# Moving two splits of returned head outputs into the last query projection, and head 0's fetches to GpSimd's queue

## The chip, the cores and the metric

The kernel runs on one core of a Trainium2 chip. The core has five engines with a queue of instructions each, which they work through in order: TensorE (PE, matrix products), VectorE (DVE), ScalarE (ACT), GpSimd (POOL) and SyncE (SP, which here only issues transfers). Transfers between HBM and the on-chip memory are issued from the queues of SP, ACT and POOL. The metric is the time of one execution on the device in microseconds, the median of several runs.

## The reference

One layer of a decoder trunk on 512 tokens of width 2048, in float32: a sparse-attention mixer with 16 heads of 128 in 4 groups, a gated feed-forward of width 5632, and three norms.

```python
def nsa_mixer(h, rel_bias, w_in, w_out, ...):
    proj = h @ w_in
    q, kc, vc, ks, vs, kw, vw, gl = jnp.split(proj, bounds, axis=-1)
    ...
    o = (gates[:, :, 0, :, :, None] * o_c + gates[:, :, 1, :, :, None] * o_s
         + gates[:, :, 2, :, :, None] * o_w)
    return o.reshape(Bsz, S, N_HEADS * DH) @ w_out

def swiglu(h, w_in, w_out):
    z = h @ w_in
    a, b = z[..., :D_FF], z[..., D_FF:]
    return (jax.nn.silu(a) * b) @ w_out

    h = x
    h = h + nsa_mixer(rmsnorm(h, mix_norm_g[0]), ...)
    h = h + swiglu(rmsnorm(h, ffn_norm_g[0]), ffn_w_in[0], ffn_w_out[0])
    return rmsnorm(h, final_norm_g)
```

The three branches of the attention (compressed, selected, window) each have a softmax per head and are summed with gates. With 8 blocks of 64 tokens and 16 to select, the selected branch takes all blocks.

## The kernel before

**Precision.** Every float32 operand of a large product is kept as two float32r parts, high and low. A *split* makes them: ScalarE copies the value into the high part, VectorE subtracts that from the value to get the low part. A product is then three matmuls (`three`, lines 266 to 269): high times high (L267), L268 and L269. At L268 one low part enters, at L269 the other. Weights are split by `Weights.split` (ScalarE L97, VectorE L98) a few tiles ahead of their use. Three raw weight tiles exist; a tile's next load is issued when its split has read it (L81).

**Stages.** First the projections of keys and values of group 0 and of the first two heads' queries. Then the attention stage (about 200 to 700 us of the span), whose outer loop runs over the 16 heads `h` with 12 steps `i` each (line 881). Then the rest of the output projection, the second norm and the feed-forward.

**The attention stage** interleaves two streams in program order, and the engines' in-order queues follow that order:

- *The head stream* (vector work mostly). For head `h + 1`, `scores` (line 781) makes the scores of one tile of 128 queries on TensorE, VectorE adds the bias and finds the maximum (L803), ScalarE takes the exponential (L805). `finish` (line 808) scales the weights by gate and sum (L810 to L817), transposes them in blocks on VectorE (L818), and stores them to HBM in four transfers (L820). `fetch(t)` (line 822) brings the tile `t` back as `PT` with the key index on the partitions (L824). For head `h`, `turn` (line 831) splits a piece of `PT` (ScalarE L841, VectorE L845 or L843), and `values` (line 848) multiplies it with the values of the head's group into `o`. `head_out` (line 861) parks the outputs of heads 0 to 11 in HBM (`d_o`, L866); from head 12 on they are split straight into the slots of `hn_h` and `hn_l` (L292, L293).
- *The dense stream* (`dense`, line 734; TensorE mostly): query, key and value projections of the coming heads and groups, and at its end four `partial` products (line 706), each of which multiplies the outputs of heads 0 to 11 with 256 columns of the output weights. `pump` (line 748) takes pieces of this stream after each step of the head stream, until a goal in TensorE time is reached; `drain_to` takes what a head needs.

Nothing else orders the work: no scheduler moves instructions. In this stage weights are loaded from GpSimd's queue (`W.queue = pool`, line 871), bias tables, stores and fetches go through SP's.

**The outputs coming back.** The normed input lies in `hn_h` and `hn_l`, 16 slots of 128 channels each. The last query projection, `qpair(14)` (line 653), runs over four chunks `i` of four slots; each chunk has two halves of four pieces, and after each piece the generator yields (`n` counts 0 to 7). When a chunk is done with, its slots are free, and `reload_o` (line 697) brings one parked output into a slot of `hn_l` from GpSimd's queue: outputs 0 to 2 in chunk 1, 3 to 5 in chunk 2, 6 to 8 in chunk 3, and 9 to 11 in the first `partial`. `split_o(k)` (line 701) splits the slots 2k and 2k + 1 in place: a copy on ScalarE (L703, 128 x 1024), then a subtraction on VectorE (L704). The `partial` products read slots 0 to 3 with their first weight tile (`i` = 0), 4 to 7 with the second and 8 to 11 with the third, each for the four token tiles `t` in turn, slot by slot.

Splits 0 and 1 stand behind the whole chunk 3 of `qpair(14)`, 2 and 3 in the first weight tile of the first `partial` ahead of its token tiles 1 and 3, and 4 and 5 in the second likewise. In program order of the time before, the copies of splits 0, 1 and 2 follow each other directly on ScalarE, behind the copy of the last query half (L292).

**The queues around head 0.** Before the loop over heads, lines 874 to 880 make the scores of head 0, tile 3 first, with `fetch(3)` and `fetch(2)` between the `finish` of the tiles; `fetch(1)` and `fetch(0)` follow in steps 0 and 2 of head 0. For later heads the fetches stand in steps 8, 11 and 2.

Of the kernel before, what the change touches and what calls it, by code (L numbers as in the profile page):

```python
# [19 lines left out]
S, D, H, DH, G, HPG = 512, 2048, 16, 128, 4, 4  # L20
# [20 lines left out]
PT_STEP = 224  # L41
# [132 lines left out]
def nsa_block(ctx: ExitStack, tc: tile.TileContext, x, rel_bias, mix_g, ffn_g, fin_g, w_in, w_out,  # L174
              pos_k, w1k, w2k, pos_v, w1v, w2v, f_in, f_out, onehot, out):
    nc = tc.nc
    mm, act, dve, pool = nc.tensor.matmul, nc.scalar.activation, nc.vector, nc.gpsimd
# [27 lines left out]
    def tok(t):  # L205
        return slice(128 * t, 128 * (t + 1))
# [59 lines left out]
    def three(o, ah, al, bh, bl, start, stop):  # L266
        mm(o, ah, bh, start=start, stop=False, skip_group_check=True)  # L267
        mm(o, ah, bl, start=False, stop=False, skip_group_check=True)  # L268
        mm(o, al, bh, start=False, stop=stop, skip_group_check=True)  # L269

    def ws(ps, gi, g, c0=0, c1=S, start=None, end=None, of=None):

        for u in range(2):
            cs = slice(128 * u, 128 * (u + 1))
            if end and gi == 3 and u:
                W.ahead(3)
            for k in range(4):
                kk = 4 * gi + k
                st = (kk == 0) if start is None else (start and kk == 0)
                three(ps[u][:, c0:c1], g[0][:, k, cs], g[1][:, k, cs],  # L280
                      *(x[:, kk, c0:c1] for x in of or (hn_h, hn_l)), st, kk == KC - 1)
                if end and gi == 3 and k == 3:
                    end(u)
                yield 650
# [57 lines left out]
    def q_out(ps, h0):  # L342
        def end(u):
            Q[h0 + u] = tuple(qp.tile([128, S], F32R, name=f"q{n}") for n in "hl")
            split_from(normed(ps[u], SCALE), Q[h0 + u][0], Q[h0 + u][1])

        return end
# [282 lines left out]
    with ExitStack() as st2:  # L630
# [3 lines left out]
        runs = [32 * (2 * t + 3) for t in range(NT)]  # L634
        P = [ap_.tile([128, 4, runs[t]], F32, name=f"p{t}", bufs=1) for t in range(NT)]
        CX = [ap_.tile([128, 32], F32, name=f"cx{t}", bufs=1) for t in range(NT)]
        PT = ap_.tile([128, 4, PT_STEP * 3 + runs[3]], F32, name="ptr", bufs=1)
        d_p = [dram.tile([4, 32, 4, runs[t]], F32, name=f"d_p{t}") for t in range(NT)]
# [5 lines left out]
        def stage_tile():  # L644
            return ap_.tile([128, 1024], F32, name="stage", bufs=1)
# [3 lines left out]
        def proj2():  # L649
            pool_ = (psx, ps2)[next(units) % 2]  # L650
            return [pool_.tile([128, 512], F32, name="proj") for _ in range(2)]

        def qpair(h0):
            ps = proj2()
            end = q_out(ps, h0)
            for i in range(4):
                last = ws(ps, i, W.take(), end=end)
                for n, c in enumerate(last):
                    yield c
                    if h0 == H - 2 and i and n in (2, 4, 6):  # L660
                        reload_o(3 * i + n // 2 - 4)
                if h0 == H - 2 and i == 3:
                    split_o(0)
                    split_o(1)
            done["n"] += 1
            yield None

# [29 lines left out]
        def reload_o(i):  # L697

            pool.dma_start(hn_l[:, i].bitcast(F32), d_o[i // 4][i % 4])

        def split_o(k):
            h, l = (x[:, 2 * k:2 * k + 2] for x in (hn_h, hn_l))
            act(h, l.bitcast(F32), AF.Copy)  # L703
            dve.tensor_tensor(l, l.bitcast(F32), h.bitcast(F32), op=OP.subtract)  # L704

        def partial(cb):
            st = stage_tile().rearrange("p (t c) -> p t c", t=NT)
            c = slice(256 * cb, 256 * (cb + 1))
            ps = [p.rearrange("p (t c) -> p t c", t=2) for p in proj2()]
            for i in range(3):  # L710
                w = W.take()
                if i == 1:
                    pool.dma_start(st, x[:, c].rearrange("(t p) c -> p t c", p=128))
                for t in range(NT):
                    if not cb and i == 0 and t < 3:
                        reload_o(9 + t)
                    if not cb and i < 2 and t % 2:
                        split_o(2 + 2 * i + t // 2)
                    if i == 2 and t == 2:
                        W.ahead(3)  # L720
                    for k in range(4):
                        h = 4 * i + k
                        three(ps[t // 2][:, t % 2], hn_h[:, h, tok(t)], hn_l[:, h, tok(t)], w[0][:, k], w[1][:, k],
                              h == 0 and t % 2 == 0, h == 11)
                        if k % 2:
                            yield 650
                    if i == 2 and t % 2:
                        b = t // 2
                        dve.tensor_tensor(st[:, 2 * b:2 * b + 2], st[:, 2 * b:2 * b + 2], ps[b], op=OP.add)
            pool.dma_start(d_h[:, c].rearrange("(t p) c -> p t c", p=128), st)  # L730
            done["n"] += 1
            yield None
# [15 lines left out]
        def pump(h, step):  # L748
            at = h + (step + 4) / STEPS
            goal = 20800 * min(at, 13) + 22500 * max(at - 13, 0)  # L750
            while done["ns"] < goal:
                c = next(stream, "end")
                if c == "end":
                    return
                done["ns"] += c or 0

        def drain_to(n):
            while done["n"] < n:
                c = next(stream, "end")
                if c == "end":  # L760
                    return
                done["ns"] += c or 0

        def needed(h):

            return 4 * ((h - 2) // 4) + (1 if h % 4 > 1 else 3) if h > 1 else 0
# [4 lines left out]
        def load_bias(h):  # L771
            if h < H:
                TB[h] = ap_.tile([128, S], F32, name="tb")
                (nc.sync if h else pool).dma_start(TB[h], bass.AP(tensor=d_u.tensor, offset=d_u.offset + h * UL + 127,
                                                 ap=[[H * UL - 1, 128], [1, S]]))
# [32 lines left out]
        def finish(h, t):  # L808
            r = HS[h]["sm"][:, t]
            dve.reciprocal(r, r)  # L810
            dve.tensor_mul(r, r, gates[:, t, h])
            for i, p in enumerate(HS[h].pop(t)):
                o = p
                if not i:
                    o = P[t][:, :3, runs[t] - 32:]
                    p = CX[t].unsqueeze(1).to_broadcast([128, 3, 32])
                dve.tensor_scalar(o, p, r[:, i:i + 1], None, op0=OP.mult)  # L817
            dve.transpose(P[t], P[t])  # L818
            for i in range(4):
                nc.sync.dma_start(d_p[t][:, :, i].rearrange("j a r -> a j r"), P[t][32 * i:32 * (i + 1)])  # L820

        def fetch(t):

            nc.sync.dma_start(PT[:, :, PT_STEP * t:PT_STEP * t + runs[t]], d_p[t].rearrange("j a i r -> (j a) i r"))  # L824

        def arrived(rows, c0, t0, step):
            v = PT[:rows, :, c0:c0 + 32]
# [46 lines left out]
        for i in range(4):  # L874
            scores(0, 3 - i)
            if i > 1:
                fetch(5 - i)
            if i:
                finish(0, 4 - i)
            pump(-1, min(9 + i, 11.7))  # L880
        for h in range(H):
            seq = [(b, kt) for kt in (3, 2, 1, 0) for b in (0, 1)] + [(-1, 0)]
            for i in range(STEPS):
                if i == 4:
                    load_bias(h + 2)
                if i == 2:
                    fetch(0)
                if i < 9:
                    turn(h, *seq[i])
                if i == 8 and h + 1 < H:  # L890
                    fetch(3)
                    fetch(2)
                if i == 11 and h + 1 < H:
                    fetch(1)
                if i == 0:
                    if not h:
                        fetch(1)
                    finish(h, 0)
                if h + 1 < H:
                    if i == 2:  # L900
                        drain_to(needed(h + 1))
                    if i % 3 == 2:
                        scores(h + 1, 3 - i // 3)
                    elif i % 3 == 0 and i:
                        finish(h + 1, 4 - i // 3)
                if 2 <= i < 10 or i == 11:
                    if i == 2 and h % HPG == 0:
                        drain_to(h)
                    values(h, *seq[min(i - 2, 8)])
                    if i == 11:  # L910
                        head_out(h)
                pump(h, i)
# [503 lines left out]
    n, na, pending = 0, 1, None  # L1416
# [88 lines left out]
```

## Time and profile before

| | us |
|---|---|
| median of 3 runs | 2143.42 (2141.70 to 2144.41) |
| profiled execution | 2139.23 |
| its span, from the first to the last instruction | 2137.5 |
| busy in it: TensorE, VectorE, ScalarE, GpSimd | 2104.2, 1634.8, 929.3, 132.5 |
| mean granted clock of TensorE | 0.994 of full speed |

A row of the profile's timeline has the start in us, the duration in us, the engine, the line of the kernel, the operation, what it writes and reads with shapes, how many like instructions are merged in the row, and in brackets the idle time of the engine before it with what ended it. "issue" there means that the profile shows no releaser. Rows of waits read: who waited for whom, us in total, how often, the longest. Rows of windows give the busy time of PE, weight loads, DVE, ACT and POOL, the granted clock, the share of the transfer engines in use and GB/s. Rows of transfers give the destination and source, the queue, the size and the median time from issue to landing. A transfer that SP issues shows as SPq.

### The profile page before, as it was taken

The page shows a single profiled execution, that of the slowest core. Times are in us where ns is not written, and L with a number is a line of the kernel's source. Part 1 is how long each engine was busy: PE and PEld are TensorE (multiplying, and loading weights), DVE is VectorE, ACT ScalarE, POOL GpSimd, SP SyncE. Part 2 cuts the span into 40 slices and gives each one's busy share as a digit, 9 for nine tenths or more (in the row PEclk, how much of TensorE's full clock was granted, in tenths as well). Part 3 has the DMA queues.
Part 4 walks back from the last instruction along what each step waited for, and adds up shares of the span by engine and source line. Part 5 has one row for each costly group of instructions (what it writes and reads, how often), then busy time and mean ns, then how long its engine had stood idle before and what let it go on. Part 6 is the DMA issues. An engine that isn't in the chain of part 4 may idle for free.

```text
span 2137.5 us, 37178 instructions
## 1 busy us (share of the span) xinstructions
PE 2104.2 (98%) x14697; PEld 1950.6 (91%) x14697; DVE 1634.8 (76%) x2674; ACT 929.3 (43%) x1439; POOL 132.5 (6%) x218
## 2 busy tenths in 40 slices
PE   9999999999989999999999999999999999999998
PEld 7898788898979889899999999999999888999896
DVE  5565777777777357898888888888888787877785
ACT  5344455555544234444444343443434444544344
POOL 1000011111121000000000000000000000001000
PEclk9999999999999999999999999999999999999999
DMA  6555667666667633344433334333343776878894
GB/s 218 177 160 152 178 191 200 193 195 192 194 214 226 229 134 113 117 131 128 129 126 122 122 125 129 129 119 127 121 129 129 258 276 219 297 268 312 300 330 153
DMA packets 272012, 388.08 MB, mean 182 GB/s; under 512 B 34668, under 2 KB 204700, under 8 KB 271197
## 3 DMA queue, kind: packets, MB, share of 16 engines
q1 hardware_dynamic: 245932, 275.52, 40.8%
q0 software_dynamic: 24000, 105.98, 14.3%
q10 hardware_dynamic: 1904, 4.20, 0.5%
q8 instruction: 115, 1.88, 0.4%
q14 instruction: 61, 0.49, 0.1%
HBM read 320.52 MB, written 70.36 MB: 183 GB/s over the span
## 4 chain that ended last, share of the span: by engine, by line
PE 65%; DMA 2%; DVE 2%; ACT 1%; issue 1%; SPq 0%; POOL 0%; ACTq 0%; DVEq 0%; POOLq 0%
PE f L268 18%; PE f L269 18%; PE f L267 18%; PE proj L269 1%; PE proj L268 1%; PE proj L267 1%; PE pp L269 1%; PE pp L268 1%; PE pp L267 1%; PE po L269 1%; PE po L267 1%; PE po L268 1%; DMA al<-d_s 1%; DMA d_p<-p 1%; DMA tt<-d_a 0%
## 5 line engine op out<-in xcount | busy, mean ns | idle before, releaser
L98 DVE TENSOR_TENSOR wlo<-raw,whi 128x1024 fp32r<-128x1024 f32 (+1 forms) x226 | 270.7, 1200 | 115.2 <-ACT whi L97 115.0
L97 ACT ACTIVATE whi<-raw 128x1024 fp32r<-128x1024 f32 (+1 forms) x226 | 234.5, 1040 | 223.6 <-DVE raw L1004 122.8
L1004 DVE TENSOR_TENSOR tlo<-tt,thi 128x1536 fp32r<-128x1536 f32 (+2 forms) x135 | 197.1, 1460 | 110.2 <-ACT thi L1106 89.0
L267 PE MATMUL f<-hn_h,whi 128*128 128x256 f32 x984 | 271.7, 276 | 0.8 <-ACT E L1064 0.8
L269 PE MATMUL f<-hn_h,wlo 128*128 128x256 f32 x984 | 271.6, 276 | 0.0
L268 PE MATMUL f<-hn_l,whi 128*128 128x256 f32 x984 | 271.6, 276 | 0.0
L1101 ACT ACTIVATE whi<-raw 128x1024 fp32r<-128x1024 f32 x123 | 126.0, 1057 | 292.2 <-DVE raw L1004 282.0
L267 PE MATMUL proj<-hn_h,whi 128*128 128x512 f32 x512 | 205.3, 401 | 0.4 <-ACT hn_h L402 0.4
L268 PE MATMUL proj<-hn_l,whi 128*128 128x512 f32 x512 | 201.5, 394 | 0.3 <-DVE hn_l L403 0.3
L269 PE MATMUL proj<-hn_h,wlo 128*128 128x512 f32 x512 | 201.5, 394 | 0.0
L267 PEld LDWEIGHTS f<-hn_h,whi 128*128 128x128 f32 x984 | 184.7, 188 | 1.2 <-ACT E L1064 1.2
L269 PEld LDWEIGHTS f<-hn_h,wlo 128*128 128x128 f32 x984 | 184.7, 188 | 0.0
L268 PEld LDWEIGHTS f<-hn_l,whi 128*128 128x128 f32 x984 | 184.7, 188 | 0.0
L1106 ACT ACTIVATE thi<-tt 128x1536 fp32r<-128x1536 f32 x82 | 121.9, 1487 | 84.2 <-PE f L268 84.2
L267 PE MATMUL proj<-whi,hn_h 128*128 128x256 f32 (+2 forms) x496 | 147.1, 297 | 6.8 <-ACT hn_h L703 6.8
L269 PE MATMUL proj<-whi,hn_l 128*128 128x256 f32 (+2 forms) x496 | 146.4, 295 | 2.9 <-DVE hn_l L704 2.9
L1004 DVE TENSOR_TENSOR wlo<-raw,whi 128x1024 fp32r<-128x1024 f32 x123 | 147.0, 1223 | 0.0
L268 PE MATMUL proj<-wlo,hn_h 128*128 128x256 f32 (+2 forms) x496 | 145.9, 294 | 0.0
L269 PE MATMUL f<-whi,tlo 128*128 128x512 f32 x320 | 124.9, 390 | 0.6 <-DVE tlo L1004 0.6
L268 PE MATMUL f<-wlo,thi 128*128 128x512 f32 x320 | 125.0, 391 | 0.0
L267 PE MATMUL f<-whi,thi 128*128 128x512 f32 x320 | 124.7, 390 | 0.0
L269 PEld LDWEIGHTS proj<-hn_h,wlo 128*128 128x128 f32 x512 | 97.0, 189 | 21.9 <-DVE wlo L98 0.2
(327 smaller groups left out, 6107.2 us busy)
## 6 DMA issues: line engine op xcount, KB each, us to landing
raw<-in_ffn_w_in SPq DMA_DIRECT2D x135, 512.0 KB, 3.6
raw<-in_ffn_w_out SPq DMA_DIRECT2D x88, 512.0 KB, 5.8
rawx<-in_ffn_w_in SPq DMA_DIRECT2D x41, 512.0 KB, 4.8
rawx<-d_a SPq DMA_DIRECT2D x31, 512.0 KB, 5.0
ah<-d_s POOLq DMA_DIRECT2D x16, 896.0 KB, 6.9
al<-d_s POOLq DMA_DIRECT2D x16, 896.0 KB, 9.5
raw<-in_nsa_w_in SPq DMA_DIRECT2D x24, 512.0 KB, 4.6
raw<-in_nsa_w_in POOLq DMA_DIRECT2D x24, 512.0 KB, 4.9
```

The costliest lines, as they stand in the source:

```text
L97: self.nc.scalar.activation(hi[:, :n], src, AF.Copy)
L98: self.nc.vector.tensor_tensor(lo[:, :n], src, hi[:, :n].bitcast(F32), op=OP.subtract)
L267: mm(o, ah, bh, start=start, stop=False, skip_group_check=True)
L268: mm(o, ah, bl, start=False, stop=False, skip_group_check=True)
L269: mm(o, al, bh, start=False, stop=stop, skip_group_check=True)
L1004: dve.tensor_tensor(o, a, b, op=OP.subtract)
L1101: act(h, r, AF.Copy)
L1106: act(h, ttf, AF.Copy)
```

## The change

```diff
@@ qpair
                     if h0 == H - 2 and i and n in (2, 4, 6):
                         reload_o(3 * i + n // 2 - 4)
-                if h0 == H - 2 and i == 3:
-                    split_o(0)
-                    split_o(1)
+                    if h0 == H - 2 and i == 3 and n in (0, 3):
+                        split_o(n // 3)
@@ partial
-                    if not cb and i < 2 and t % 2:
+                    if not cb and i < 2 and t % 2 == 0:
                         split_o(2 + 2 * i + t // 2)
@@ fetch
-        def fetch(t):
-
-            nc.sync.dma_start(PT[:, :, PT_STEP * t:PT_STEP * t + runs[t]], d_p[t].rearrange("j a i r -> (j a) i r"))
+        def fetch(t, queue=nc.sync):
+
+            queue.dma_start(PT[:, :, PT_STEP * t:PT_STEP * t + runs[t]], d_p[t].rearrange("j a i r -> (j a) i r"))
@@ the scores of head 0, and the loop over heads
             if i > 1:
-                fetch(5 - i)
+                fetch(5 - i, pool)
...
                 if i == 2:
-                    fetch(0)
+                    fetch(0, nc.sync if h else pool)
...
                     if not h:
-                        fetch(1)
+                        fetch(1, pool)
```

Splits 0 and 1 are issued inside chunk 3 of the last query projection, after its pieces 0 and 3. Splits 2 to 5 are issued one token tile earlier in the first `partial`, at its token tiles 0 and 2. The four fetches of head 0 are issued from GpSimd's queue, in the same places of the program; there they stand among the weight loads of line 81, which are issued in the same stage. All other fetches stay on SP's queue. No work is added or removed, and TensorE's instructions keep their order.

## The prediction

> **What bounds the kernel now.** I read the busy times first, then TensorE's waits by name, then the stretch that holds the longest of them, engine by engine in order of time.
>
> ```profile
> span 2137.5 us, 37178 instructions
> PE 2104.2 (98%) x14697; PEld 1950.6 (91%) x14697; DVE 1634.8 (76%) x2674; ACT 929.3 (43%) x1439; POOL 132.5 (6%) x218
> ...
> PE proj L267 <- ACT hn_h L703: 6.8, 2, 6.2
> PE proj L269 <- DVE hn_l L704: 2.9, 2, 2.1
> ```
>
> TensorE is busy 98% of the span, so a change can gain only its idle 2137.5 - 2104.2 = 33.3 us, plus time in which it runs slowly. The largest named waits are the two that the change aims at: 6.8 + 2.9 = 9.7 us for the splits of lines 703 and 704. Two more waits, 2.58 and 0.84 us (rows below), belong to head 0, whose fetches move.
>
> The stretch with the splits on TensorE, then its clock there (columns: PE, PEld, DVE, ACT, POOL busy, granted clock, DMA share, GB/s):
>
> ```profile
> 611.66 0.58 PE L267 MATMUL proj<-whi,hn_h 128*128 128x256 f32 x1 [6.22 <-ACT hn_h L703]
> 614.55 0.58 PE L269 MATMUL proj<-whi,hn_l 128*128 128x256 f32 x1 [2.09 <-DVE hn_l L704]
> 619.40 0.28 PE L267 MATMUL proj<-whi,hn_h 128*128 128x256 f32 x1
> 625.52 0.39 PE L269 MATMUL proj<-whi,hn_l 128*128 128x256 f32 x1 [0.76 <-DVE hn_l L704]
> 632.93 0.28 PE L269 MATMUL proj<-whi,hn_l 128*128 128x256 f32 x1
> 641.65 0.44 PE L268 MATMUL o<-ptl,v1h 128*128 128x384 f32 x1 [0.21 <-DVE ptl L845]
> ...
> 606.00:612.00 6.00, 0.34 (x1) 0.34 (x2) 4.88 (x15) 4.28 (x11) 3.41 (x6) 0.76 0.77 270
> 612.00:618.00 6.00, 3.91 (x18) 3.62 (x18) 4.73 (x6) 1.50 (x2) 0.00 (x0) 0.50 1.03 368
> ```
>
> TensorE is through with the last query projection at 611.66 - 6.22 = 605.4, stands still to 611.7 for split 0, again to 614.6 for its low part, and then runs at half clock (0.50) until 619.4. While it stands still, VectorE is busy 4.88 of 6 us: that queue is what the splits must pass.
>
> **The change part by part.** Edit 1 adds and removes no work: the same six copies and six subtractions come earlier in the in-order queues of ScalarE and VectorE. TensorE's own order stays as it is. What each displaces must be followed there:
>
> ```profile
> 604.89 0.63 ACT L292 ACTIVATE qh<-yt 128x512 fp32r<-128x512 f32 x1 [4.00 <-DVE yt L319]
> 605.43 1.04 ACT L97 ACTIVATE whi<-raw 128x1024 fp32r<-128x1024 f32 x1
> ...
> 603.58 0.68 DVE L845 TENSOR_TENSOR ptl<-ptr,pth 128x512 fp32r<-128x512 f32 x1
> 604.17 0.68 DVE L319 SCALAR_TENSOR_TENSOR yt<-proj,ybc 128x512 f32<-128x512 f32 x1
> 606.50 1.23 DVE L98 TENSOR_TENSOR wlo<-raw,whi 128x1024 fp32r<-128x1024 f32 x1 [0.25 <-ACT whi L97]
> 613.31 3.45 DVE L704 TENSOR_TENSOR hn_l<-hn_l,hn_h 128x1024 fp32r<-128x1024 f32 x3
> 621.36 0.19 DVE L803 CUSTOM_DVE_ANT_0 cx<-s,biasc 128x31 f32<-128x31 f32 x1 [4.60 <-PE s L269]
> 629.74 1.22 DVE L704 TENSOR_TENSOR hn_l<-hn_l,hn_h 128x1024 fp32r<-128x1024 f32 x1
> 631.38 0.43 DVE L845 TENSOR_TENSOR ptl<-ptr,pth 128x256 fp32r<-128x256 f32 x1 [0.42 <-issue]
> ```
>
> *Split 0* now stands before the L845 of 603.58. Its subtraction costs 3.45 / 3 = 1.15 there, so L845 starts at 604.73 and TensorE's matmul on it waits about 0.6 us; L319 starts at 605.32. TensorE enters the partial product at 605.9 without waiting for split 0.
>
> *Split 1* follows the L292 that L319 releases. L292 started 0.72 after L319 (604.89 - 604.17) and released ScalarE 0.54 later (605.43 - 604.89): 605.32 + 0.72 + 0.54 = 606.58, the copy (1.04, as the one of equal size at 605.43) ends at 607.62, the subtraction starts at 607.65. TensorE got going 1.24 after such a start (614.55 - 613.31), so here at 608.89.
>
> *What is pushed back.* Behind split 1, L98 starts at 607.65 + 1.15 = 608.80 instead of 606.50: 2.30 later, and so do the end of the last query projection and the finishing of head 13's second tile, which lie on VectorE up to 613.31. Split 2's subtraction therefore starts at 613.31 + 2.30 = 615.61, and TensorE, which would be there at about 614.4 (45 matmuls after 608.89 at 0.12, the mean of the 60 or so between 625.52 and 632.93), waits to 616.85. Also behind that L98 stands GpSimd's queue:
>
> ```profile
> 597.09 1.60 POOL L699 DMA_DIRECT2D hn_l<-d_o  x3
> 608.02 0.76 POOL L81 DMA_DIRECT2D raw<-in_nsa_w_out  x1 [2.55 <-DVE wlo L98]
> 608.77 2.66 POOL L699 DMA_DIRECT2D hn_l<-d_o  x5
> ...
> hn_l<-d_o POOLq DMA_DIRECT2D x1, 256.0 KB, 5.3
> ...
> L699 POOL DMA_DIRECT2D hn_l<-d_o x12: 537/539/552, 589.7 to 610.9; - x12
> ...
> DMA to landing us min/median/max: 4.5/5.9/7.1
> ```
>
> Outputs 2 and 3, which split 1 reads, are issued by 598.7 at the latest and landed 7.1 later at most, 605.8: no wait. The weight load of 608.02 waits for L98, and the last five reloads queue behind it. Output 7 goes out at 608.77 + 2.30 = 611.07 and lands 5.3 later, at 616.37 (4.5 to 7.1: 615.6 to 618.2). *Split 3* needs it: its copy ends at 617.45, its subtraction starts at 617.50, TensorE passes at 618.74. The copy now waits on ScalarE ahead of the exponentials of head 13's last tile and of head 12's output, and VectorE ahead of their first step (L803): a late output 7 holds them all, one for one. Before, this matmul ran at 625.52: 6.8 us gained, for the moment.
>
> *Splits 4 and 5.* VectorE's L803 follows split 3 at 617.50 + 1.15 = 618.65. From L803 to the L845 of 631.38 it took 10.02; without the idle 0.42 there and without split 3's subtraction inside (1.15) it takes 8.45. So L845 starts at 627.10 and split 5's subtraction 1.22 earlier, 625.88; TensorE has its result 1.24 later, at 627.12, where it would have been at 618.74 + (632.93 - 625.52) = 626.15: a wait of 1.0, and a lead of 632.93 - 627.12 = 5.8. VectorE itself leads by 631.38 - 627.10 = 4.3 only. At 641.65 TensorE already waited 0.21 for VectorE, so there its lead falls to VectorE's. Edit 1: **-4.3 us**. Where the stall goes: out of TensorE's 605 to 619, partly into new waits at splits 1, 2, 3 and 5 and at that L845.
>
> Its bounds: output 7 one way or the other gives -4.3 - 0.7 (split 3 right behind split 2, at 616.76) to -4.3 + 1.8. A clock that drops again after 618.74 is a rival below.
>
> *Edit 2*, head 0's fetches. Columns of the engine rows as above; SPq is the sync queue's issue:
>
> ```profile
> 216.46 1.11 DVE L818 STREAM_TRANSPOSE p<-p 128x896 f32<-128x896 f32 x1
> 218.50 0.61 SPq L824 DMA_DIRECT2D ptr<-d_p  x1
> 219.21 2.00 SPq L820 DMA_DIRECT2D d_p<-p  x4
> 223.99 0.44 PE L267 MATMUL o<-pth,v0h 128*128 128x128 f32 x1 [2.58 <-issue]
> 229.18 0.42 ACT L841 ACTIVATE pth<-ptr 128x256 fp32r<-128x256 f32 x1 [5.09 <-DMA ptr<-d_p]
> 237.57 0.44 PE L268 MATMUL o<-ptl,v0h 128*128 128x384 f32 x1 [0.84 <-DVE ptl L845]
> 246.45 1.04 ACT L97 ACTIVATE whi<-raw 128x1024 fp32r<-128x1024 f32 x1
> 224.00:227.00 3.00, 3.00 (x9) 2.50 (x10) 1.88 (x8) 0.09 (x1) 0.00 (x0) 0.50 0.64 206
> ```
>
> The first fetch waits on the sync queue for its stores, and the next tile's four stores, ready at 217.57, go out only at 219.21. With the fetch on GpSimd's queue they go out 1.6 us earlier, and the second fetch, which waits for them, as well; what waited for it at 229.18 moves up by 1.6 too, which covers the 0.84 us that TensorE waits at 237.57. The first fetch gains nothing: its own stores set its start. It costs what a GpSimd issue costs over a sync issue:
>
> ```profile
> tb<-d_u POOLq DMA_DIRECT2D x1, 256.0 KB, 3.4
> ...
> tb<-d_u SPq DMA_DIRECT2D x1, 256.0 KB, 3.9
> ...
> raw<-in_nsa_w_in SPq DMA_DIRECT2D x1, 256.0 KB, 2.9
> ...
> raw<-in_nsa_w_in POOLq DMA_DIRECT2D x1, 256.0 KB, 4.4
> ...
> L81 POOL DMA_DIRECT2D raw<-in_nsa_w_in x68: 747/749/764, 221.5 to 566.6; - x68
> ```
>
> The same table row took 0.5 less from GpSimd, a weight load 1.5 more; the tiles fetched here are nearer to the first pair in shape, the load around them nearer to the second: I take 0, bounds -0.5 to +1.5. The weight loads queued behind the second fetch on GpSimd go out some 2 us later (about 223.6), land within 4.4, and are first read by the third copy from there, at 246.45: free, with 18 us of cover; without it they would cost their delay one for one. Edit 2: **-0.8 us**, from -1.3 to +0.7.
>
> [...]
>
> Sum: -4.3 - 0.8 = -5.1 us. The profiled execution took 2139.23 us (span and 1.7 around it), 4.2 below the median of 2143.42; the terms are differences inside it, so they go onto the median: **2138.3 us**.
>
> **The rivals.** *B, half the gain is given back* (0.21). The pauses before 616.85 and 618.74 add up to about 3.7 us within 4.4; one pause of 2.58 before 223.99 was enough for a clock of 0.50. If the clock falls for as long as at 611.66 to 619.40 (7.7 us, at 0.5 about half the work, 3.6 us lost), TensorE is at 626.15 + 3.6 = 629.75 instead; the lead is 632.93 - 629.75 = 3.2, and with edit 2 at nothing the time is 2140.2. A late output 7 (618.2) comes to 2140.9. Against: TensorE follows VectorE here, so slow matmuls are mostly hidden.
> [...]
>
> *C, more is gained* (0.08): with output 7 early (-0.7) and head 0's pause short enough that the clock holds (half clock from 224 to 230 costs about 2.8): 2143.4 - 5.0 - 0.8 - 2.8 = 2134.8.
>
> [...]
>
> **How the numbers follow.** Forecast 0.62, B 0.21, C 0.08, D 0.09. About 0.2%, 4.3 us, is what a measurement of this kernel can tell from no change, so "faster" means below 2139.1. The forecast lies only 0.8 beyond that: of its 0.62 I put 0.50 below and 0.12 above. Faster 0.50 + 0.08 = 0.58; same 0.12 + 0.21 = 0.33; slower 0.09. The range goes from C, 2134.8, to B with its late output and edit 2 at its dear end, 2143.4 - 2.5 + 0.7 = 2141.6, and on both sides takes in the spread of the runs (2141.70 to 2144.41, so 1.7 below and 1.0 above their median) and a little of D: 2133.0 to 2143.0.
>
> **What would show it.** Right: no wait of line 267 on line 703 near 605; waits of about 1 us at split 1, 2.4 at split 2, 1.3 at split 3; output 7 landing near 616.4; a lead of some 4 us at 641.65; head 0's second tile read by ScalarE near 227.6, and no wait at 237.57. Wrong: GpSimd issues over 0.8 us, a pause before 223.99 much over 2.6, output 7 later than 620, or half clock after 619.

## The result and the profile after

| | median, us | runs | ratio to before, 95% interval |
|---|---|---|---|
| before | 2142.19 | 2136.99 to 2146.26 (16) | |
| after | 2133.49 | 2130.71 to 2142.80 (16) | 0.9966 [0.9953, 0.9978] |
| after, measured a second time (before then 2139.64) | 2138.43 | 2128.76 to 2144.64 (12) | 0.9976 [0.9960, 0.9993] |

By these ratios the change makes the kernel faster by 0.34% and 0.24%, that is 7.3 and 5.1 us; the forecast was 5.1. A ratio is not that of the two medians beside it, which lie 8.7 and 1.2 us apart: the runs of one kernel spread over some 10 us, those of the changed kernel over 12 and 16. So the sizes of the parts are read below from the traces, by matching each of the 14697 matmuls of one profile with the same one of another.

TensorE's waits between 200 and 760 us of the changed kernel (who waited for whom, us in total, times, longest):

```profile
span 2131.3 us, 37171 instructions
...
PE o L268 <- DVE ptl L844: 4.5, 5, 2.9
...
PE proj L269 <- DVE hn_l L703: 1.7, 3, 0.8
...
PE proj L267 <- ACT hn_h L702: 0.9, 2, 0.5
```

(From line 663 on, numbers are one lower than before: L702 and L703 are the splits, L844 was L845.) The waits for the splits fell from 9.7 to 2.6 us. In their place TensorE waits 4.5 us for VectorE's turned weights (1.8 before), 2.9 of it at one matmul. The stretch in order of time, TensorE first, then what stands before it on VectorE and ScalarE:

```profile
603.85 0.50 PE L268 MATMUL o<-ptl,v1h 128*128 128x512 f32 x1 [2.90 <-DVE ptl L844]
606.06 0.58 PE L267 MATMUL proj<-whi,hn_h 128*128 128x256 f32 x1 [0.45 <-ACT hn_h L702]
607.32 0.58 PE L269 MATMUL proj<-whi,hn_l 128*128 128x256 f32 x1 [0.47 <-DVE hn_l L703]
615.56 0.38 PE L269 MATMUL proj<-whi,hn_l 128*128 128x256 f32 x1 [0.52 <-DVE hn_l L703]
616.77 0.38 PE L267 MATMUL proj<-whi,hn_h 128*128 128x256 f32 x1 [0.47 <-ACT hn_h L702]
618.02 0.39 PE L269 MATMUL proj<-whi,hn_l 128*128 128x256 f32 x1 [0.76 <-DVE hn_l L703]
...
597.86 0.69 DVE L844 TENSOR_TENSOR ptl<-ptr,pth 128x512 fp32r<-128x512 f32 x1 [3.84 <-ACT pth L840]
...
603.11 0.69 DVE L844 TENSOR_TENSOR ptl<-ptr,pth 128x512 fp32r<-128x512 f32 x1
...
606.04 1.23 DVE L703 TENSOR_TENSOR hn_l<-hn_l,hn_h 128x1024 fp32r<-128x1024 f32 x1 [0.25 <-ACT hn_h L702]
607.18 1.22 DVE L98 TENSOR_TENSOR wlo<-raw,whi 128x1024 fp32r<-128x1024 f32 x1
...
614.33 1.18 DVE L703 TENSOR_TENSOR hn_l<-hn_l,hn_h 128x1024 fp32r<-128x1024 f32 x1
616.75 1.22 DVE L703 TENSOR_TENSOR hn_l<-hn_l,hn_h 128x1024 fp32r<-128x1024 f32 x1 [1.24 <-ACT hn_h L702]
...
626.15 0.42 DVE L844 TENSOR_TENSOR ptl<-ptr,pth 128x256 fp32r<-128x256 f32 x1
...
597.20 0.63 ACT L840 ACTIVATE pth<-ptr 128x512 fp32r<-128x512 f32 x1 [2.31 <-DMA ptr<-d_p]
...
604.97 1.04 ACT L702 ACTIVATE hn_h<-hn_l 128x1024 fp32r<-128x1024 f32 x1
...
615.65 1.06 ACT L702 ACTIVATE hn_h<-hn_l 128x1024 fp32r<-128x1024 f32 x1 [3.37 <-DMA hn_l<-d_o]
```

Two transfers show here that the prediction had not placed so. Output 7 comes at 615.65 (split 3's copy waits 3.37 us for it), and head 12's last tile, fetched from the sync queue, comes late at 597.20: VectorE stands idle for 3.84 us before its L844, where it stood 1.42 before (its L845 at 599.46 there). Those 2.42 us push everything behind it.

Head 0, TensorE's one pause and the clock behind it (columns as in the prediction's windows):

```profile
222.44 0.44 PE L267 MATMUL o<-pth,v0h 128*128 128x128 f32 x1 [3.00 <-issue]
```

```profile
222.50:225.90 3.40, 3.40 (x10) 2.79 (x11) 2.55 (x12) 0.61 (x3) 0.75 (x1) 0.50 0.90 271
226.00:229.40 3.40, 3.40 (x20) 2.91 (x19) 1.98 (x9) 3.15 (x9) 0.00 (x0) 1.00 0.43 137
604.80:611.60 6.80, 5.89 (x27) 5.30 (x26) 5.45 (x12) 4.90 (x12) 2.90 (x6) 0.50 0.50 149
618.40:621.80 3.40, 3.40 (x19) 3.40 (x18) 1.84 (x4) 3.40 (x11) 0.00 (x0) 0.50 0.37 116
```

The pause is 3.00 us, but half clock ends after 3.4 us, where it had lasted through the whole of 224 to 230 before, and the wait of 0.84 us some 13 us later is gone.

### The profile page after: what moved, and what is told of

Read it like the earlier page. It is cut to its first block, busy times and chain, and to the rows that moved or that the text cites. A ratio compares the mean times of both kernels' runs of the same rounds, so it can differ in the third digit from the quotient of the medians.

```text
span 2131.3 us, 37171 instructions
## 1 busy us (share of the span) xinstructions
PE 2103.4 (99%) x14697; PEld 1950.5 (92%) x14697; DVE 1634.7 (77%) x2674; ACT 928.8 (44%) x1439; POOL 135.2 (6%) x222
## 4 chain that ended last, share of the span: by engine, by line
PE 66%; DMA 1%; DVE 1%; ACT 1%; issue 0%; SPq 0%; ACTq 0%; DVEq 0%
PE f L267 19%; PE f L268 19%; PE f L269 19%; PE proj L267 1%; PE proj L268 1%; PE proj L269 1%; PE pp L267 1%; PE pp L268 1%; PE pp L269 1%; PE po L267 1%; PE po L268 1%; PE po L269 1%; DMA d_p<-p 1%; DMA rawx<-d_a 0%; PE pp L245 0%
## 5 line engine op out<-in xcount | busy, mean ns | idle before, releaser
L98 DVE TENSOR_TENSOR wlo<-raw,whi 128x1024 fp32r<-128x1024 f32 (+1 forms) x226 | 270.7, 1200 | 115.6 <-ACT whi L97 115.4
```

Of the source, the lines that this page charges most:

```text
L98: self.nc.vector.tensor_tensor(lo[:, :n], src, hi[:, :n].bitcast(F32), op=OP.subtract)
```

## The experiments

All ran on the chip beside the kernel before. This table, for all fourteen profiles of the case, gives by how much the same matmul came later (+) or earlier than in the first profile of before: as offset at the start of the attention stage (205), and as the change of that offset over head 0 (205 to 260), around the splits (593 to 645) and over the last head's end (645 to 800). "Tile late" is VectorE's idle time before its first full L844 of head 12 (the row at 597.86) less the 1.42 us of before.

```
profile                         start  head 0  splits  tile late  splits less that  last head
before                           0      0       0       0          0                 0
before_again                    -1.4   +1.6    -0.6    +0.1       -0.7              +1.8
e10_before_sp                   -2.1   +1.0    +0.2     0         +0.2              -1.4
e2_fetch_only                   -2.0   -1.9    +3.4    +3.2       +0.2              +2.1
e4_splits01_only                -2.3   -0.3    -1.8    +0.2       -2.0              +0.8
e5_splits25_only                -1.9   +0.1    +4.6    +6.1       -1.6              -0.3
e1_splits_only                  -1.9   -0.1    +2.1    +6.0       -3.9              -0.3
after                           -2.0   -2.3    -1.2    +2.4       -3.6              +0.3
after_again                     -2.0   -0.5    -0.9    +3.1       -4.0              +4.9
e3_first_fetch_sp               -2.2   +1.6    -4.3     0         -4.3              +3.7
e7_x_sp                         -1.7   -2.3    +1.8    +5.7       -3.9              -1.2
e6_reload_sp                    -1.7   -0.8    -5.1     0         -5.1              +5.8
e8_x_and_reload_sp              -0.3   -1.1    -5.2     0         -5.2              -1.4
e9_split0_early                 -1.8   -2.1    -4.5     -          -                -1.2
```

The start is 1.4 to 2.3 us earlier in all but one of them, the second profile of before included: the first one had begun late, ahead of every instruction that the change moves.

The splits can also be read without taking off the late tile, in VectorE's rows: from that first L844 to the L844 that carries the lead (626.15 in the changed kernel, 631.38 before) it took 31.2 to 32.2 us in the four profiles with all splits as before, 29.87 in e4, 30.35 in e5, 27.7 to 28.3 in the five with the six splits moved as in the change and the returning outputs on GpSimd's queue, and 26.7 and 26.6 in e6 and e8.

### The two edits apart, and the change again

e1 is the changed kernel with all fetches on the sync queue:

```diff
-                fetch(5 - i, pool)
+                fetch(5 - i)
...
-                    fetch(0, nc.sync if h else pool)
+                    fetch(0)
...
-                        fetch(1, pool)
+                        fetch(1)
```

> The splits are moved as in the change, all fetches stay on the sync queue. Theory (the splits pay VectorE's lead, some 4 us, whatever head 0 does): 3.5 to 4.5 us faster than before (ratio 0.9979 to 0.9984), TensorE's wait for the copies of the splits falls from 6.8 to about 1 us, and head 0 looks as before (pause of about 2.6 us before the first product with values, 0.84 us wait some 13 us later). Rival (most of the gain is head 0's clock and scatter): within 1.5 us of before, though the waits at the splits are gone.

Measured: 2135.40 us beside 2139.64 before, ratio 0.9978 [0.9967, 0.9990], so 4.7 us. In its profile TensorE waits 0.8 us for the copies of the splits, down from 6.8, and 3.7 for their subtractions, up from 2.9. Head 0 takes the time of before, but not in the way expected: the wait near 237 is 1.9 us instead of 0.84, and no half clock follows the pause. The splits bring 3.9 us there once the late tile (6.0 us in this execution) is taken off. The theory holds.

e2 is the changed kernel with the splits where they were:

```diff
-                    if h0 == H - 2 and i == 3 and n in (0, 3):
-                        split_o(n // 3)
+                if h0 == H - 2 and i == 3:
+                    split_o(0)
+                    split_o(1)
...
-                    if not cb and i < 2 and t % 2 == 0:
+                    if not cb and i < 2 and t % 2:
```

> The four fetches of head 0 on GpSimd's queue, the splits as before. Theory: 0.8 us faster from the wait that vanishes, up to 3 us where the half-clock spell behind head 0's pause is also shorter (as in the profile of the changed kernel: 3.5 us of it in place of 6); the 6.2 and 2.1 us waits at the splits stay. [...] Rival (the gain at head 0 in one profile was chance): within 0.5 us of before, half clock for 6 us again.

Measured: 2137.44 us, ratio 0.9989 [0.9974, 1.0003], some 2.4 us, an interval that just reaches no change. In head 0 it gains 1.9 us: no wait near 237, and behind a pause of 3.0 us a spell of half clock of 3.4 (its window):

```profile
223.20:226.70 3.50, 3.50 (x11) 2.85 (x11) 2.35 (x11) 0.83 (x3) 0.75 (x1) 0.51 0.90 276
```

Its splits are as before (waits of 7.2 and 2.9 us), later by the late tile alone.

The changed kernel, once more:

> The changed kernel once more, on the same chip as its two halves. Theory: the two halves add up: the time before, plus both differences, within 1 us, so 5 to 7.5 us faster than before. Rival (the halves share a slack): less than their sum by over 1.5 us. Its second profile shows how far the pause before head 0's values (3.0 us), the half-clock spell behind it (3.5 us) and the late arrival of head 12's first tile (2.4 us lost) vary from one execution to the next: chance if they differ by more than 1 us, the kernel's own if not.

The two halves' 4.7 and 2.4 add up to 7.1, against 7.3 and 5.1 for the whole. The 5.1, measured beside them, is 2.0 less than their sum, which was the rival's condition; but its interval alone goes from 1.5 to 8.6 us, so the times do not decide it. In the traces the two parts lie in separate stretches, and each has there about the size that it has alone: -3.6 and -4.0 at the splits beside e1's -3.9, and -2.1 and -1.6 from 205 to 593 beside e2's -1.9. The second profile shows what varies: the half clock in head 0 lasts 6.8 us this time, and head 12's tile is 3.1 us late. What is the kernel's own is that none of the seven profiles with head 0's four fetches on GpSimd has a wait near 237, while the other seven all have one, of 1.9 us in five of them. Over head 0, the seven with them average -1.6 us (-2.3 to -0.5), and the six with all fetches on the sync queue +0.4 (-0.3 to +1.6): about 2 us for edit 2. Followed on from 205 to 593 the two groups part more clearly, since the two that lose most in head 0 (before_again and e10) win it back before 500: -1.7 on average (-2.2 to -1.2) against 0.0 (-0.8 to +0.9).

e3 is the changed kernel with one line different:

```diff
-                fetch(5 - i, pool)
+                fetch(5 - i, nc.sync if i == 2 else pool)
```

> The changed kernel with head 0's first fetch back on the sync queue, where the next tile's four stores stand behind it; the other three fetches on GpSimd's queue. Theory (what pays in head 0 is that these stores no longer wait): the stores go out 1.6 us later again, the 0.84 us wait is back, and the time is 0.8 to 2.5 us longer than the changed kernel's. Rival (what pays is the other three fetches, or a quicker landing from GpSimd's queue): the same as the changed kernel within 0.5 us, or faster by up to 0.4 us, since the pause before the first values shrinks from 3.0 to 2.6.

Measured: ratio 0.9979 [0.9968, 0.9991], which can't be told from the changed kernel's. The trace tells: the sync queue's rows, then TensorE's.

```profile
216.27 0.60 SPq L823 DMA_DIRECT2D ptr<-d_p  x1
216.99 4.43 SPq L819 DMA_DIRECT2D d_p<-p  x8
...
221.53 0.30 PE L267 MATMUL o<-pth,v0h 128*128 128x128 f32 x1 [2.33 <-issue]
235.69 0.44 PE L268 MATMUL o<-ptl,v0h 128*128 128x384 f32 x1 [1.92 <-DVE ptl L844]
```

With the first fetch again ahead of the next tile's stores, these go out behind it, and the wait near 237 is back (1.92 us) with a second spell of half clock; head 0 takes 1.6 us more than before. The pause shrinks to 2.33, as the rival had it, but that buys nothing. What pays in edit 2 is the sync queue that the first fetch no longer blocks.

### The limits that are left

The next three runs move transfers that stand in the way of others around 600 and 700. e6 is the changed kernel with the returning outputs on the sync queue:

```diff
-            pool.dma_start(hn_l[:, i].bitcast(F32), d_o[i // 4][i % 4])
+            nc.sync.dma_start(hn_l[:, i].bitcast(F32), d_o[i // 4][i % 4])
```

> The changed kernel with the twelve returning outputs fetched from the sync queue, so that they no longer stand behind a weight load which waits for VectorE. Theory (split 3 is late only because output 7 was issued behind that load at 608.7, and head 12's last tile only because three returning outputs went out ahead of it): output 7 lands before 614, split 3's copy does not wait for a transfer (3.37 us before), TensorE's wait at split 3 (0.8 to 2.5 us) is gone, and the fetch of head 12's last tile lands within 3.2 us of its issue; VectorE's lead grows by 1 to 1.5 us, and the time is 1 to 2 us below the changed kernel's, ratio to before 0.9960 to 0.9972. Rival (the returning outputs then wait on the sync queue for free slots and hold head 13's stores and fetches): those are issued 1 to 4 us later and the time is the changed kernel's or more.

Measured: 2131.00 us beside 2138.52, ratio 0.9964 [0.9952, 0.9976]. Around the splits 5.1 us are gained. Why head 12's tile is late is seen by comparing e1's issues (GpSimd's queue, then the sync queue) with those of e8, which has the same move of the returning outputs as e6:

```profile
593.73 0.76 POOL L81 DMA_DIRECT2D raw<-in_nsa_w_out  x1 [5.01 <-DVE wlo L98]
594.47 1.60 POOL L698 DMA_DIRECT2D hn_l<-d_o  x3
...
594.93 0.53 SPq L823 DMA_DIRECT2D ptr<-d_p  x1
```

The tile's fetch in e1 goes out behind a weight load of 512 KB and among three outputs of 256 KB; transfers of that window, with their size and the time from issue to landing:

```profile
hn_l<-d_o POOLq DMA_DIRECT2D x3, 256.0 KB, 6.0
raw<-in_nsa_w_out POOLq DMA_DIRECT2D x1, 512.0 KB, 4.2
ptr<-d_p SPq DMA_DIRECT2D x1, 192.0 KB, 7.2
```

And e8:

```profile
593.45 0.53 SPq L823 DMA_DIRECT2D ptr<-d_p  x1
...
594.90 0.75 POOL L81 DMA_DIRECT2D raw<-in_nsa_w_out  x1 [6.73 <-DVE wlo L98]
```

```profile
raw<-in_nsa_w_out POOLq DMA_DIRECT2D x1, 512.0 KB, 6.4
hn_l<-d_o SPq DMA_DIRECT2D x1, 256.0 KB, 2.8
ptr<-d_p SPq DMA_DIRECT2D x1, 192.0 KB, 2.8
```

192 KB took 7.2 us in the one and 2.8 in the other. In all ten profiles with the outputs on GpSimd's queue the tile is in time (landing within 3.0 us) when its issue comes ahead of that weight load, as in four of them, and late (4.4 to 7.2) when it comes behind, as in six. Both before and after the change these issues lie within 2 us of each other, and neither edit moves an instruction right ahead of them, so I take it for a matter of the execution. That is not shown: with the outputs on GpSimd's queue the tile is late in all four profiles that have the whole of edit 2 (e2, e7 and the two of the changed kernel), and in two of the six others (e1 and e5). So it comes without edit 2, but that the change makes it more frequent is open. In the four profiles with the outputs on the sync queue the tile is in time. The theory holds for the splits: output 7, issued at 601.68, lands 6.3 us later, and split 3's copy does not wait for it. But the profile of e6 then loses 5.8 us over the last head; its execution took 2134.45 us, the second longest of twelve.

e7 is the changed kernel with the input slices of `partial` on the sync queue:

```diff
-                    pool.dma_start(st, x[:, c].rearrange("(t p) c -> p t c", p=128))
+                    nc.sync.dma_start(st, x[:, c].rearrange("(t p) c -> p t c", p=128))
```

> The changed kernel with the input slices of the partial products (512 KB each) fetched from the sync queue; the last of them then goes out behind the last head's last stores instead of among them. Theory (near 700 us the last head's last fetch decides, because its stores land behind that slice: 7.4 us against 4 to 5): those stores land within 5.5 us, TensorE's waits from 697 to 706 (1.4 us in one profile of the changed kernel, 3.3 in the other, besides slower clock behind them) fall below 0.7, and the time is 1 to 3 us below the changed kernel's. Rival (the slice, now later, holds VectorE's addition instead, which waits 2.1 us for it already): VectorE waits 4 us or more for the slice and the time is the same or more.

Measured: 2131.60 us, ratio 0.9964 [0.9949, 0.9979]. The last head's stores and its last fetch, in the changed kernel and, in the second fence, here:

```profile
688.23 2.00 SPq L819 DMA_DIRECT2D d_p<-p  x4
688.71 0.77 POOL L712 DMA_DIRECT2D stage<-in_x  x1
...
696.96 0.52 SPq L823 DMA_DIRECT2D ptr<-d_p  x1
```

```profile
691.30 1.99 SPq L819 DMA_DIRECT2D d_p<-p  x4
693.34 0.45 SPq L712 DMA_DIRECT2D stage<-in_x  x1
696.87 0.53 SPq L823 DMA_DIRECT2D ptr<-d_p  x1
```

From the first store to the fetch, which waits for all four to land, it was 8.7 us and is 5.6 (in the ten profiles without this move 8.0 to 9.8, in the four with it 5.5 to 6.2). Between 690 and 710 TensorE waits 0.3 us in all, where the changed kernel's two profiles have 1.4 and 3.0; VectorE waits 1.3 us for the input slice, less than the 2.1 in the changed kernel, so the rival falls. The changed kernel's third store, issued behind the slice, shows where the time went (transfers around 689.3):

```profile
stage<-in_x POOLq DMA_DIRECT2D x1, 512.0 KB, 7.8
d_p<-p SPq DMA_DIRECT2D x1, 48.0 KB, 7.4
```

48 KB land when the 512 KB issued 0.6 us earlier do (688.71 + 7.8 = 696.5, 689.31 + 7.4 = 696.7). That does not hold for each store: the second one, issued at 688.83 while GpSimd was still issuing the slice, landed 5.2 us later, at 694.0 and so before it. What holds the third one back for 7.4 us, no run here shows.

e8 makes both moves in the changed kernel.

> Both of the moves of the two runs above in the changed kernel: returning outputs and input slices from the sync queue. Theory (two separate limits, around 605 to 620 and around 700): the gains add up, 2 to 4 us below the changed kernel, ratio to before 0.9945 to 0.9965. Rival (only the later limit counts, since the lead won at the splits is lost near 700 anyway): the same as with the input slices alone, within 0.7 us. Second rival (the sync queue becomes the bound): slower than the changed kernel.

Measured: 2129.19 us (2127.87 to 2130.05 in 6 runs) beside 2138.52, ratio 0.9954 [0.9939, 0.9968]. It gains 5.2 us at the splits and keeps it (-1.4 over the last head): by its ratio it lies 1.2 and 2.2 thousandths below the changed kernel's two (with intervals that overlap), and its runs spread over 2 us instead of 12 and 16. The two limits are separate: e6 lost near 700 what it had won, and e7 still lost at 597. Both profiles are of long executions, though (e7's, at 2136.77, is the longest of seven), so they show what can still happen, not what does as a rule.

The kernel before, once more:

> The kernel before once more, for a second profile of it. Theory: TensorE's waits at splits 0 and 1 (6.8 and 2.9 us in the first profile) and head 0's pause and 0.84 us wait come again within 0.3 us, for they follow from the order of the queues; the 2.0 us wait for the input at the very start, which all later profiles showed as 0.5 to 1.6, is chance and will differ. If the waits at the splits differ by more than 1 us as well, then the differences of single profiles there say little.

Its profile waits 6.9 and 2.9 us at the splits, within 0.1 us of the first one. The wait near 237 did not come again within 0.3: it is 1.9 us instead of 0.84, with a second spell of half clock, so the first profile of before had shown edit 2's wait nearly at its shortest (e4 has 0.65).

### The parts of edit 1, and two more bases

e4 and e5 are the kernel before with splits 0 and 1 alone moved, and with splits 2 to 5 alone moved (the lines of e2's diff, one group each).

> The kernel before with splits 0 and 1 alone moved into the last query projection; splits 2 to 5 one token tile later, as before, and all fetches on the sync queue. Theory (the end is set by VectorE's queue): most of the splits' gain, 3 to 4.5 us between 593 and 645 where head 12's last fetch is in time, since these two lie in front of TensorE's 9.7 us of waits; TensorE then waits 1 to 2.5 us at split 3, which stands later. Rival (the gain needs all six): under 1.5 us there.

Measured: 0.9990 [0.9976, 1.0004], and in the profile 2.0 us at the splits: less than the 3 to 4.5 of the theory, more than the rival's 1.5. The wait for split 0 is gone and split 1 costs 0.8 twice, but split 3 now holds TensorE, 12 us later, and its clock falls (the window's third number from the end):

```profile
617.75 0.58 PE L267 MATMUL proj<-whi,hn_h 128*128 128x256 f32 x1 [2.02 <-ACT hn_h L702]
...
627.16 0.42 DVE L844 TENSOR_TENSOR ptl<-ptr,pth 128x256 fp32r<-128x256 f32 x1 [2.71 <-issue]
```

```profile
617.10:624.00 6.90, 5.78 (x25) 5.49 (x26) 6.53 (x13) 4.14 (x7) 1.51 (x2) 0.51 0.67 200
```

VectorE then stands idle for 2.71 us before the L844 at 627.16, without a releaser on the page; that it waits there for slow TensorE to free `ptl` is my reading of the code, not shown.

> The kernel before with splits 2 to 5 alone one token tile earlier; splits 0 and 1 behind the query projection as before, and all fetches on the sync queue. Theory: the waits of 6.8 and 2.9 us at splits 0 and 1 stay; split 2, which already stood right behind them, gains nothing, and the time between 593 and 645 stays within 1 us of before. Rival (the earlier token tile is what pays): 2 us or more.

Measured: 0.9990 [0.9978, 1.0002]; 1.6 us at the splits in the profile, net of a tile that was 6.1 late. My theory gave these four nothing, and neither it nor its rival names the size. VectorE's rows show where it comes from: the subtractions of splits 0 to 3 follow each other (618.43, 4.59 us in one piece), where split 3's had stood behind the wait of L803 for TensorE's scores (4.60 us before, at 621.36; 3.62 here). The parts add: 2.0 + 1.6 = 3.6, against 3.6 to 4.3 for all six. So the four splits that this document's title leaves out carry a good part. Split 0 frees TensorE, but the lead is kept only if the later splits move with it.

e9 is e8 with split 0 earlier:

```diff
-                    if h0 == H - 2 and i == 3 and n in (0, 3):
-                        split_o(n // 3)
+                    if h0 == H - 2 and (i, n) in ((2, 6), (3, 3)):
+                        split_o(i - 2)
```

> The changed kernel with returning outputs and input slices on the sync queue, and split 0 after piece 6 of chunk 2 instead of piece 0 of chunk 3. There VectorE stands idle for 1.42 us (at 596.5 in the profile of the kernel with both moves), so its subtraction no longer pushes the rest of VectorE's queue back. Theory (VectorE's lead sets the end): 1.1 us less than with both moves, ratio to before 0.9940 to 0.9955, TensorE's first product with the turned weights not delayed. Rival (copy of split 0 on ScalarE delays the copy behind it, or the lead is lost near 700): same within 0.5 us or slower.

Measured: 2130.52 us, ratio 0.9954 [0.9942, 0.9966]: the same as e8, and 0.7 us less gained at the splits in the profile. The rival holds:

```profile
595.87 1.04 ACT L702 ACTIVATE hn_h<-hn_l 128x1024 fp32r<-128x1024 f32 x1
596.81 0.62 ACT L840 ACTIVATE pth<-ptr 128x512 fp32r<-128x512 f32 x1
...
596.94 1.23 DVE L703 TENSOR_TENSOR hn_l<-hn_l,hn_h 128x1024 fp32r<-128x1024 f32 x1 [1.85 <-ACT hn_h L702]
```

The copy takes ScalarE at 595.87, when it would otherwise have read head 12's tile (L840, now at 596.81). VectorE now waits 1.85 us for the copy where it had waited 1.42 for L840: its idle time there was ScalarE's doing, and work that begins on ScalarE can't fill it.

e10 is the kernel before with the two moves of e8.

> The kernel before, with returning outputs and input slices on the sync queue and nothing else: the base on which the change stands without the two transfers that vary. Theory (the change's two parts are worth some 4.3 and 2 us, and the two moves help the changed kernel because they let it keep that): TensorE still waits 6 us or more at split 0, for VectorE's queue and not for a transfer, and the time is 5 to 7 us above the kernel with both moves, ratio to before 0.998 to 1.001. Rival (late transfers were the larger part of the waits at the splits): the waits fall below 4 us and the ratio below 0.997.

Measured: 2136.40 us, ratio 0.9987 [0.9977, 0.9997]. The two waits at the splits stay whole:

```profile
PE proj L267 <- ACT hn_h L703: 6.9, 2, 6.2
PE proj L269 <- DVE hn_l L704: 2.9, 2, 2.1
```

So they come from VectorE's queue, not from transfers, and the rival falls. On this base the change is worth 0.9954 / 0.9987 = 0.9967, 7 us, good to some 4 (the intervals are 0.15% and 0.1% wide to each side); the traces say 7.5: 5.4 at the splits (from +0.2 to -5.2) and 2.1 in head 0 (from +1.0 to -1.1). The twelve runs of e10 still spread over 9 us, where the six of e8 spread over 2, so in the kernel before something besides these two transfers varies from run to run; what it is, its one profile does not show.

## Why the prediction was right, and where it was off

*Edit 1, the queue.* The prediction followed VectorE instruction by instruction; set on the time that L844 started (603.11, where it had 604.73, so 1.62 less), its numbers against the rows above are:

| step | predicted | measured |
|---|---|---|
| split 1's copy | 604.96 | 604.97 |
| split 1's subtraction | 606.03 | 606.04 |
| L98 behind it | 607.18 | 607.18 |
| split 2's subtraction | 613.99 | 614.33 |
| output 7 issued, landed | 609.45, 614.75 | 609.45, 615.57 |
| split 3's subtraction | 615.88 | 616.75 |
| the L844 that carries the lead | 625.48 | 626.15 |

The order of the queues was right to a few hundredths up to L98. Split 2's subtraction is 0.3 late behind 0.37 us in which VectorE stands idle before L816 (612.72); what it waits for there, the profile does not name. The term that was mis-sized is output 7's landing: 5.3 us after its issue was predicted, 6.1 measured, inside the bounds of 4.5 to 7.1:

```profile
hn_l<-d_o POOLq DMA_DIRECT2D x1, 256.0 KB, 6.1
```

That is the 0.7 us between 4.3 and the 3.6 found. In e3, where the tile is in time and output 7 takes 5.5 us, the gain is the predicted 4.3. That this landing held the splits is shown by e6, where output 7 does not wait behind the weight load: 5.1. That the lead falls to VectorE's is borne out by the stretch's gain staying at VectorE's 3.6 to 4.3 us in five of the changed profiles.

*The waits that were to come.* At split 1 they add up to 0.45 + 0.47 = 0.9 us (1.0 predicted), at split 3 to 0.47 + 0.76 = 1.2 (1.3), but at split 2 to 0.5 where 2.4 was predicted: TensorE ran at half clock from 604.8 to 611.6 and came there later by itself. In e8, where no such spell lies ahead of it, the wait is 2.1. What the prediction missed is the wait of 2.9 ahead of them all, for which it had 0.6: the late tile. It took the tile's landing from one profile as given, though that fetch is in a race with GpSimd's weight load.

*Rival B.* Its condition came true, and with it a sign of being wrong that the prediction had named, half clock after 619. Its price did not: the clock fell at 604.8 and 618.4 (windows above), for 3.4 us the second time and not 7.7, and the net gain was 3.6 of 4.3, since VectorE set the pace. In e4 a spell of 6.8 us from 617.1 went with a smaller gain, 2.0; how much of that is the clock's is not shown.

*Edit 2.* Right in kind, too small: 0.8 predicted, about 2 found. The wait that vanishes was read as 0.84 from one profile, but is 1.9 in five of seven, and a shorter spell of half clock adds to it in some profiles. This had been counted only in rival C. Head 0's second tile was read at 224.73 instead of 229.18; with the start 1.97 earlier that is 2.5 us sooner, where 1.6 was predicted. The fetch's own price was put at 0 and is not: the pause grew by 0.42 us, and in all fourteen profiles it is 2.16 to 2.79 with the first fetch on the sync queue and 2.98 to 3.37 with it on GpSimd's. That lies inside the stated -0.5 to +1.5.

*D*, the 0.09 for slower and a little of the range, is borne out by no run. The sign named for it, GpSimd issues over 0.8 us, did not show: head 0's four fetches in the changed kernel (duration minimum, median, maximum in ns) are

```profile
L823 POOL DMA_DIRECT2D ptr<-d_p x4: 747/755/766, 217.1 to 229.8; - x4
```

*The sum.* 5.1 predicted, 7.3 and 5.1 measured. Both terms have the right sign and place; edit 1 gave 0.7 less and edit 2 about 1 more, so that the errors partly cancel, and the late tile then took 2.4 and 3.1 us off in the two profiles of the changed kernel. That the times fit so well is in part luck. The median of 2133.49 lies 4.8 below the forecast of 2138.3 and 0.5 inside its range; it is nearer to rival C's 2134.8, but what C supposed, an output 7 that comes early and a shorter pause, did not happen. The second median, 2138.43, is the forecast's almost to the digit, but from 2139.64 and not from the 2143.42 of three runs on which the forecast stood.

## What to carry to other kernels

A wait on an in-order queue is moved by following that queue instruction by instruction; here this gave the starts of the first 4 us to within 0.03. A lead lasts until the next transfer that has no slack (e6 won 5.1 us at the splits and lost 5.8 over the last head): before believing a gain, look for the short transfers behind long ones further on, and issue the long one after them (here 192 KB took 7.2 us behind a load of 512 KB in e1, and 2.8 ahead of it in e8). One profile does not tell whether a gap of 1 us in a wait is the kernel's or the execution's; two profiles of the kernel before would have told here.

## What was unexpected in the hardware

*Half clock came in pieces of 3.4 us.* In fourteen profiles its spells between 200 and 720 us last 3.4, 6.8, 10.2 or 13.7 us, and the stretches at full clock between them are whole multiples of 3.41 us as well (in the kernel before 208.2 us is 61 of them, and 378.9 is 111). Pauses of 2.16 to 3.37 us before head 0's first values brought one in thirteen of them; in e1 a pause of 2.47 did not (the granted clock is the third number from the end):

```profile
220.00:228.00 8.00, 5.01 (x22) 3.67 (x22) 2.29 (x9) 0.93 (x3) 1.16 (x2) 1.00 0.82 243
```

The length of the pause does not tell how many pieces follow: 6.8 us of half clock with a pause of 2.58 us in the kernel before, 3.4 with 3.00 and 6.8 with 3.4 in the two profiles of the changed kernel, none with 2.47 in e1. What decides it, the traces do not show.

*A short transfer paid for a long one on another queue:* 192 KB took 2.8 or 7.2 us and 48 KB 4.1 or 7.4, by whether a load of 512 KB from another queue had been issued just before (e1 and e8; the third store of the changed kernel and, without such a load, the second of e8).
